# Sixteen groups of transposes read float32r copies made by DMAs, in a one-core decoder trunk

## The chip, the core and the metric

The kernel runs on one core of a Trainium2 chip. The metric is the device time of one execution in microseconds (us). The kernel before took 1412.33 us, the median of three runs (1411.7 to 1413.66). One core's engines work side by side, each through its own instructions in its own order: TensorE (PE, with its weight loads as PEld), VectorE (DVE), ScalarE (ACT), GpSimd (POOL) and SyncE (SP). In this kernel SP and POOL issue the DMAs. An instruction starts when the one before it on its engine has been issued and the data that it needs are there.

## What is computed

The reference is a trunk of two layers over 512 tokens of width 1024, all in float32. Each layer is a token mixer, a normalization, an MLP with a squared ReLU, a second normalization and a gate:

```python
for i in range(DEPTH):                       # DEPTH = 2
    mix = ssd_mixer(x, ...) if i % 2 == 0 else hgrn2_mixer(x, ...)
    h = layer_norm(DEEPNORM_ALPHA * x + mix, ln_g[i, 0], ln_b[i, 0])
    h = layer_norm(DEEPNORM_ALPHA * h + sq_relu_mlp(h, mlp_w1[i], mlp_w2[i]), ln_g[i, 1], ln_b[i, 1])
    x = h + jax.nn.sigmoid(h @ ple_w_gate[i]) * (p[i] @ ple_w_proj[i])
```

Both mixers begin with a projection of x and end with an output projection; the MLP is 1024 to 4096 to 1024.

## The kernel before

**Rows and columns.** The running state is the tile `acc`: for each of four chunks of 128 tokens, one row block of 128 partitions (tokens) by 1024 channels in float32. Norms and gates work on row blocks, since their sums go along the channels. The matrix products that follow need the channels on the partitions, so every normalized row block is transposed on TensorE: eight 128x128 squares for each chunk, four into one PSUM bank at a time. Such a group of four, with one identity matrix (`ident`, a slice of the constants `cst`), is what the profile shows as one row `pt<-cst,acc ... x4`. From the bank, ACT copies the group to the high part of a split operand and DVE takes the rest.

**Split products.** Every float32 product is made of three float32r ones (`mm3`, L120 to L122): both operands are split into a float32r high part (`hi`, by an ACT copy that rounds) and a float32r rest (`lo`, by a DVE subtraction). The profile writes `f32` for both types on TensorE; what is float32r there has `whi`, `wlo` or `b` (the tag `b8`) as its operands, what is float32 has `cst`, `acc`, `xw`, `qd` and the like.

**The norms in front of the MLPs.** `norm(0)` follows the first layer's output projection, `norm(2)` the second's. `out_project` goes chunk by chunk: two halves of the product (`out_part`, DVE adds each into `acc`, L260 or its like), then `after(c)`, which is `layer_norm`: statistics (L207, L208 in `norm(0)`), then two passes over the whole row block, `(x - mean) * g` (L223) and `* rs + b` (L224). Then `transpose_split` transposes the row block in two groups (L238), each followed by the ACT copy (L242) and the DVE subtraction (L243). The transposes of chunk c stand on TensorE in the middle of the products of the next chunk. `norm(1)` and `norm(3)` stand in front of the gates and go through the same `transpose_split`.

**The gate of the first layer** goes by halves h of the channels and chunks c. For each (h, c) there are 24 products into a bank, a sigmoid on ACT, a multiplication and the addition into `acc` on DVE (L666). The sum is the second layer's input, so it is transposed too: `turn(h, c)` (L625) is put off by one block through the list `late`, that is, it stands on TensorE behind the products of the next block. The last one, `turn(1, 3)`, is handed to the second layer's first products.

**What sets the order.** The program is written in a high-level order and a scheduler places each instruction on its engine's queue; `tc.high_priority(offset=...)` (the constants SOON = 40, LEAD = 100) moves pieces ahead. Tiles come from pools by tag; a tag has as many buffers as the phase's table says (`ssd`, `mlp0`, `hgrn`, `mlp1`), one where it says nothing. A new tile in a used buffer waits for the readers of the old one.

**POOL's queue.** POOL does almost nothing but issue DMAs: the loads of weight blocks `r` (`weight_sums`, L329), 512 KB each, in eights. The first eight of each MLP are the first blocks that DVE adds and subtracts (L336 and its neighbours) for the products of the first MLP group. SP's queue loads all other weights (`raw`).

Of the kernel before, what the change touches and what calls it, by code (L numbers as in the profile page):

```python
# [9 lines left out]
F32R = mybir.dt.float32r  # L10
# [5 lines left out]
P = 128  # L16
T = 512
# [27 lines left out]
def trunk(ctx: ExitStack, tc, a):  # L45
    nc = tc.nc
    pool = lambda name, bufs, **kw: ctx.enter_context(tc.tile_pool(name=name, bufs=bufs, **kw))
    cpool = pool("consts", 1)
# [15 lines left out]
    def nm(s):  # L64
        uid[0] += 1
        return f"{s}_{uid[0]}"

    def mk(p, shape, tag, dt=F32, **kw):
        return p.tile(list(shape), dt, tag=tag, name=nm(tag), **kw)

    def f32(t):
        return t.bitcast(F32)
# [16 lines left out]
    def tmp(tag, shape, dt=F32):  # L89
        return mk(phase[0], shape, tag, dt, bufs=phase[2].get(tag, 1))  # L90

    def bank(p, tag):
        return mk(p, [P, T], tag)
# [8 lines left out]
    def unit(src, lead=LEAD, after=None):  # L102
        n = src.shape[1]
        with tc.high_priority(offset=lead):
            raw = mk(raws, [P, 1024], "raw")
            nc.sync.dma_start(raw[:, :n], src)
        return split(raw[:, :n], lead, after)
# [39 lines left out]
    acc = mk(accp, [P, NCH, D], "acc")  # L147
# [32 lines left out]
    ident, triu, eps = cols["ident"], cols["triu"], cols["eps"]  # L180
    convw = cols["convw"].rearrange("p (i k) -> p i k", k=4)
    convb, dskip, snw, hlb, hnw = (cols[n] for n in ("convb", "dskip", "snw", "hlb", "hnw"))
    dtc = cols["dtc"]
    ones = tmp("cm", [P, P])
    nc.gpsimd.memset(ones, 1.0)
    one = mk(cpool, [P, 1], "one")
    nc.gpsimd.memset(one, 1.0)
    ones_s = mk(cpool, [P, 64], "ones_s")
    nc.gpsimd.memset(ones_s, 1.0 / 512)


    def ln_params(i):
        g = mk(w4, [P, D], "a")
        b = mk(w4, [P, D], "b")
        nc.sync.dma_start(g, a["ln"][2 * i : 2 * i + 1, :].to_broadcast([P, D]))
        nc.sync.dma_start(b, a["ln"][2 * i + 1 : 2 * i + 2, :].to_broadcast([P, D]))
        return g, b

    def layer_norm(i, c, gb, sums=None):

        src = acc[:, c, :]
        mv = mk(sm, [P, 2], "lnmv")
        sd = mk(sm, [P, 1], "lnsd")
        if sums is None:
            st = mk(sm, [P, 2, 6], "lnst")
            for h in range(2):
                nc.vector.bn_stats(st[:, h, :], src[:, h * 512 : (h + 1) * 512])  # L207
            nc.vector.bn_aggr(mv, st.rearrange("p a b -> p (a b)"))  # L208
            nc.scalar.activation(sd, mv[:, 1:2], AF.Sqrt, bias=eps)
        else:  # L210

            sq = mk(sm, [P, 2], "lnsq")
            nc.vector.tensor_scalar(mv[:, 0:1], sums[:, c, 0:1], sums[:, c, 1:2], -1.0 / D, ALU.add, ALU.mult)
            for h in range(2):
                nc.scalar.activation(
                    tmp("cbm" if i == 2 else "sg", [P, T]), src[:, h * 512 : (h + 1) * 512], AF.Square, bias=mv[:, 0:1], accum_out=sq[:, h : h + 1]
                )
            nc.vector.tensor_add(mv[:, 1:2], sq[:, 0:1], sq[:, 1:2])
            nc.scalar.activation(sd, mv[:, 1:2], AF.Sqrt, scale=1.0 / D, bias=eps)
        rs = mk(sm, [P, 1], "lnrs")  # L220
        nc.vector.reciprocal(rs, sd)
        shift = ALU.subtract if sums is None else ALU.add
        nc.vector.scalar_tensor_tensor(src, src, mv[:, 0:1], gb[0], shift, ALU.mult)  # L223
        nc.vector.scalar_tensor_tensor(src, src, rs, gb[1], ALU.mult, ALU.add)  # L224
# [3 lines left out]
    def behind(ins):  # L228
        return tc.issue_after(ins.ins) if ins is not None else nullcontext()

    def transpose_split(src, dst, c, apart, keep=None):

        sl = slice(c * P, (c + 1) * P)
        for q in range(2):
            pt = bank(psm, "pm") if (c == 3 if keep is not None else apart and q) else bank(pst, "pt")
            for j in range(4):
                k = 4 * q + j
                nc.tensor.transpose(pt[:, j * P : (j + 1) * P], src[:, k * P : (k + 1) * P], ident)  # L238
            v = pt.rearrange("p (j t) -> p j t", j=4)
            h = dst.hi[q][:, :, sl]  # L240
            with tc.high_priority(offset=LEAD if apart or keep is not None else SOON):
                nc.scalar.copy(h, v)  # L242
                turned_last[:] = [nc.vector.tensor_sub(dst.lo[q][:, :, sl], v, f32(h))]  # L243
                if keep is not None and q == 0:
                    nc.scalar.copy(keep[:, c // 2, :, c % 2 * P : (c % 2 + 1) * P], v)
            yield
# [38 lines left out]
    def norm(i, keep=None):  # L285

        gb = ln_params(i)
        h_s = Split(8)
        sums = mk(sm, [P, NCH, 2], "lnsum") if i else None

        def chunk(c):
            with tc.high_priority(offset=LEAD if c == 3 and i % 2 == 0 else 0 if c > 1 and i == 1 else SOON):
                layer_norm(i, c, gb, sums)

        return h_s, chunk, lambda c: transpose_split(acc[:, c, :], h_s, c, c == 3 and i % 2 == 0, keep), sums

# [259 lines left out]
    def mlp_and_gate(layer, h_s, last):  # L558
# [36 lines left out]
        for g, period in enumerate(PERIODS):  # L595
            if g < 4:
                tiles = hidden(g)
            if g > 0:
                if g == 4:
                    kept = tmp("blk", [P, 2, 4, 256]) if last else None  # L600
                    h_s, after, turned, sums = norm(2 * layer + 1, kept)
# [15 lines left out]
        rows = [tmp("blk", [P, 2, 4, 256]) for _ in range(2)]  # L617
        late = []

        def turn(h, c):  # L620

            sl = slice(c * P, (c + 1) * P)
            pt = bank(pst, "pt")
            for j in range(4):
                nc.tensor.transpose(pt[:, j * P : (j + 1) * P], acc[:, c, h * 512 + j * P : h * 512 + (j + 1) * P], ident)  # L625
            v = pt.rearrange("p (j t) -> p j t", j=4)
            hh = x_n.hi[h][:, :, sl]
            nc.scalar.copy(hh, v)
            nc.scalar.copy(rows[c // 2][:, h, :, c % 2 * P : (c % 2 + 1) * P], v)
            nc.vector.tensor_sub(x_n.lo[h][:, :, sl], v, f32(hh))  # L630
# [3 lines left out]
        def proj(c, pu):  # L634

            ps = pps[c] = bank(*((psj, "pj") if c > 1 and pps else (psy, "py%d" % (c % 2))))
            sl = slice(c * P, (c + 1) * P)
            for k in range(2):
                ks = slice(k * 512, (k + 1) * 512)
                mm3(ps, p_s[0][:, k, sl], p_s[1][:, k, sl], pu[0][:, ks], pu[1][:, ks], k == 0, k == 1)  # L640

        for h in range(2):
            pu = unit(a[f"wp_{layer}"][h])
            gu = [unit(a[f"wg_{layer}"][4 * h + j]) for j in range(4)]
            for c in range(NCH):
                sl = slice(c * P, (c + 1) * P)
                if h == c == 0:
                    turns = turned(1)
                    for i in range(NCH):
                        proj(i, pu)  # L650
                        if i in (1, 2):
                            next(turns)
                if h == 1:
                    proj(c, pu)
                turns = turned(c + 2) if h == 0 and c < 2 else None
                pg = bank(psj, "pj")
                sg = tmp("sg", [P, T])
                for k in range(8):
                    ks = slice((k % 2) * 512, (k % 2 + 1) * 512)
                    mm3(pg, h_s.h(k, sl), h_s.l(k, sl), gu[k // 2][0][:, ks], gu[k // 2][1][:, ks], k == 0, k == 7)  # L660
                    if turns and k in (2, 5):
                        next(turns)
                nc.scalar.activation(sg, pg, AF.Sigmoid)
                nc.vector.tensor_mul(sg, pps.pop(c), sg)
                d = acc[:, c, h * 512 : (h + 1) * 512]
                nc.vector.tensor_add(d, sg, d)  # L666
                while late:
                    late.pop(0)()
                late.append(lambda h=h, c=c: turn(h, c))
        return x_n, rows, late  # L670

    def values4(xs, rows, late):
# [297 lines left out]
    for j in range(17):  # L970
# [6 lines left out]
        if pend is not None:  # L977
            i = j - 1
# [27 lines left out]
    x_s, rows, late = mlp_and_gate(0, h_s, False)  # L1006
# [98 lines left out]
    def need(*key):  # L1105
        while key not in made:
            next(bg)
        return made[key]
# [218 lines left out]
    with tc.manual_schedule(engines={mybir.EngineType.PE}):  # L1327
        for h in range(0, 8, 2):
            if h % 4 == 0:
                halves.append(Split(4))  # L1330
            if h == 0:
                need("qf", 1)
                fill(AHEAD)
            scale = 1.0 if h < 6 else LAST
            for n in hcore(h, halves[-1], h % 4):
                fill(n * scale)
        for _ in bg:
            pass
    h_s, *after = norm(2)
    out_project(a["who"][4:8], halves[1], False, *after)  # L1340
    begin("mlp1")
    mlp_and_gate(1, h_s, True)
    phase[1].__exit__(None, None, None)

# [119 lines left out]
```

## Time and profile before

| | |
|---|---|
| device time, three runs | 1411.7, 1412.33, 1413.66 us |
| span of the profiled execution | 1409.6 us, 2.7 us under the median; the page has no other time of that execution |
| PE busy | 1404.3 us, 100%, 8001 instructions |
| DVE busy | 1069.1 us, 76% |
| ACT busy | 763.6 us, 54% |
| POOL busy | 45.8 us, 3%, 92 instructions |
| DMA | 181.69 MB, mean 129 GB/s |

How to read it: a row of a timeline gives an instruction's start and its duration in us, its engine and line, what it writes and reads, and the shapes. Matmuls are pipelined, so their durations overlap, and the distance between two starts is what one costs. The norms' transposes in question lie near 356 to 366 us and 1008 to 1018 us of the span, the gate's between 721 and 766 us.

### The profile page before, as it was taken

Reading aid. Unit: us, or ns where it says so; the run is one execution under the profiler, and the core shown is the slowest. Engines: PE = TensorE matmul, PEld = TensorE weight load, DVE = VectorE, ACT = ScalarE, POOL = GpSimd, SP = SyncE. Lnnn points to the kernel's source line nnn. Section 1 sums busy time; section 2 is a strip of 40 time slices with the busy share of each in tenths; the row PEclk is TensorE's granted clock in tenths of the full one; section 3 lists DMA queues with packets and bytes.
Section 4 is the critical chain, followed back from the end, with each engine's and each line's share of the span. In section 5 each row is a group of like instructions: output and inputs, shape, how many; then the busy total and the mean of one; then the engine's idle time right before and its main releaser. Section 6 shows DMA issues by size and latency. Waiting matters only on the chain.

```text
span 1409.6 us, 20400 instructions
## 1 busy us (share of the span) xinstructions
PE 1404.3 (100%) x8001; PEld 1168.1 (83%) x8001; DVE 1069.1 (76%) x1778; ACT 763.6 (54%) x1156; POOL 45.8 (3%) x92
## 2 busy tenths in 40 slices
PE   9999999999999999999999999999999999999998
PEld 7888888888988888888888888888898888888887
DVE  7989688698977668677986577678785867667795
ACT  7766465573354444545555547655555454544573
POOL 0000000001000000000000000000100000000100
PEclk9999999999999999999999999999999999999999
DMA  8433333234433444345621421222443444444731
GB/s 313 135 117 120 106 120 110 85 100 156 141 113 127 157 131 152 129 142 178 209 90 49 134 91 61 76 87 96 150 135 105 147 137 148 144 137 159 202 106 60
DMA packets 50399, 181.69 MB, mean 129 GB/s; under 512 B 5632, under 2 KB 6400, under 8 KB 50176
## 3 DMA queue, kind: packets, MB, share of 16 engines
q1 hardware_dynamic: 38784, 138.45, 29.6%
q0 software_dynamic: 11520, 41.95, 9.2%
q8 instruction: 63, 1.03, 0.3%
q14 instruction: 32, 0.26, 0.1%
HBM read 177.16 MB, written 2.16 MB: 127 GB/s over the span
## 4 chain that ended last, share of the span: by engine, by line
PE 99%; DMA 0%; DVE 0%; issue 0%; DVEq 0%
PE pj L120 25%; PE pj L121 25%; PE pj L122 25%; PE py L120 5%; PE py L122 5%; PE py L121 5%; PE py L906 1%; PE pt L238 1%; PE py L1175 1%; PE pm L923 1%; PE pm L871 1%; PE py L1301 1%; PE pt L859 0%; PE py L1303 0%; PE py L1240 0%; PE py L832 0%
## 5 line engine op out<-in xcount | busy, mean ns | idle before, releaser
L113 ACT CAST whi<-raw 128x1024 fp32r<-128x1024 f32 x218 | 228.8, 1050 | 333.2 <-PE pj L121 243.6
L120 PE MATMUL pj<-b,whi 128*128 128x512 f32 (+1 forms) x990 | 378.6, 383 | 0.0
L122 PE MATMUL pj<-b,wlo 128*128 128x512 f32 (+1 forms) x990 | 376.8, 381 | 0.0
L121 PE MATMUL pj<-b,whi 128*128 128x512 f32 (+1 forms) x990 | 376.6, 381 | 0.0
L116 DVE TENSOR_TENSOR wlo<-raw,whi 128x1024 fp32r<-128x1024 f32 x218 | 265.4, 1221 | 129.4 <-ACT whi L113 128.2
L121 PEld LDWEIGHTS pj<-b,whi 128*128 128x128 f32 x990 | 186.4, 188 | 34.6 <-issue 0.9
L122 PEld LDWEIGHTS pj<-b,wlo 128*128 128x128 f32 x990 | 186.3, 188 | 34.5
L120 PEld LDWEIGHTS pj<-b,whi 128*128 128x128 f32 x990 | 186.1, 188 | 34.0
L122 PE MATMUL pj<-whi,b 128*128 128x512 f32 x520 | 204.1, 392 | 0.0
L120 PE MATMUL pj<-whi,b 128*128 128x512 f32 x508 | 202.1, 398 | 0.0
L121 PE MATMUL pj<-wlo,b 128*128 128x512 f32 x508 | 199.2, 392 | 0.0
L113 ACT CAST whi<-r 128x1024 fp32r<-128x1024 f32 x76 | 80.0, 1053 | 68.5 <-PE pj L122 39.4
L122 PEld LDWEIGHTS pj<-whi,b 128*128 128x128 f32 x520 | 97.7, 188 | 20.1
L120 PEld LDWEIGHTS pj<-whi,b 128*128 128x128 f32 x508 | 95.5, 188 | 19.1 <-ACT b L1322 0.3
L121 PEld LDWEIGHTS pj<-wlo,b 128*128 128x128 f32 x508 | 95.5, 188 | 18.7 <-issue 0.2
L116 DVE TENSOR_TENSOR wlo<-r,whi 128x1024 fp32r<-128x1024 f32 x76 | 92.5, 1220 | 19.6 <-ACT whi L113 19.1
L122 PE MATMUL py<-whi,b 128*128 128x512 f32 x260 | 101.3, 390 | 0.0
L121 PE MATMUL py<-wlo,b 128*128 128x512 f32 x248 | 96.6, 389 | 0.0
L120 PE MATMUL py<-whi,b 128*128 128x512 f32 x248 | 96.4, 390 | 0.0
L329 POOL DMA_DIRECT2D r<-in_w x64 | 34.0, 532 | 1098.8 <-DVE wlo L116 544.3
L122 PEld LDWEIGHTS py<-whi,b 128*128 128x128 f32 x260 | 48.8, 188 | 10.2
L800 DVE SCALAR_TENSOR_TENSOR cv<-pj,cst,cv 128x509 f32<-128x509 f32 (+2 forms) x66 | 48.9, 746 | 10.6 <-ACT cv L797 9.8
(368 smaller groups left out, 1943.5 us busy)
## 6 DMA issues: line engine op xcount, KB each, us to landing
raw<-in_w SPq DMA_DIRECT2D x112, 512.0 KB, 3.3
r<-in_w POOLq DMA_DIRECT2D x64, 512.0 KB, 3.8
raw<-in_wssd SPq DMA_DIRECT2D x36, 512.0 KB, 3.9
a<-csd SPq DMA_DIRECT2D x16, 512.0 KB, 4.1
raw<-in_wso SPq DMA_DIRECT2D x16, 512.0 KB, 3.3
raw<-in_whq SPq DMA_DIRECT2D x16, 512.0 KB, 3.4
raw<-in_wg SPq DMA_DIRECT2D x15, 512.0 KB, 4.0
raw<-in_whvg SPq DMA_DIRECT2D x14, 512.0 KB, 3.4
```

The costliest lines, as they stand in the source:

```text
L113: nc.scalar.copy(hi[:, :n], f)
L116: nc.vector.tensor_sub(lo[:, :n], f, f32(hi[:, :n]))
L120: nc.tensor.matmul(out, sh, mh, start=start, stop=False, **kw)
L121: nc.tensor.matmul(out, sh, ml, start=False, stop=False, **kw)
L122: return nc.tensor.matmul(out, sl, mh, start=False, stop=stop, **kw)
L238: nc.tensor.transpose(pt[:, j * P : (j + 1) * P], src[:, k * P : (k + 1) * P], ident)
L329: queue.dma_start(t[i][u], src)
L800: nc.vector.scalar_tensor_tensor(cv[:, d:], ps[:, : T - d], convw[:, i, k : k + 1], cv[:, d:], ALU.mult, ALU.add)
L871: nc.tensor.matmul(pst_[:, c * P : (c + 1) * P], btok[:, c, :], xw[:, c].rearrange("p h q -> p (h q)"), start=True, stop=True)
L906: mm = nc.tensor.matmul(yds[0][64 * r : 64 * r + 64, sl], xdt[:, 2 * c + r, :], m[:, r, sl], start=True, stop=True)
L923: mm = nc.tensor.matmul(yo[:, c * P : (c + 1) * P], pv[:, c - 1].rearrange("p h q -> p (h q)"), cm[:, c * P : (c + 1) * P], start=True, st ...
L1175: nc.tensor.matmul(pcs[r][bs, at : at + n], kk[r][:, ts], qs, start=True, stop=True)
```

## The change

Sixteen of the groups of four transposes read another tile. They are the groups of chunks 0 and 1 behind `norm(0)` and `norm(2)` (two for each chunk, eight in all) and the eight groups of the first layer's gate. As soon as the float32 half row block (128x512, 256 KB) is final in `acc`, a DMA on POOL's queue copies it within SBUF into a tile of type float32r, with the bits unchanged (`same_bits`). The transposes read that tile, with an identity that POOL has cast to float32r (`rounded`), and write float32r into the PSUM bank; the ACT copy and the DVE subtraction behind them are as before. Chunks 2 and 3 of these norms and the norms in front of the gates are transposed from `acc` in float32, as before. The copies of the norms go to tag `xs` (four buffers in both phases), those of the gate to a new tag `xr`, which has one buffer.

```diff
+    def rounded(tag):
+        t = tmp(tag, [P, P], F32R)
+        nc.gpsimd.tensor_copy(t, ident)
+        return t
+
+    def same_bits(tag, src):
+        t = tmp(tag, [P, T], F32R)
+        nc.gpsimd.dma_start(f32(t), src)
+        return t
+
+    eye = [rounded("identr")]
...
-    ones_s = mk(cpool, [P, 64], "ones_s")
+    ones_s = tmp("ones_s", [P, 64])
...
-    def transpose_split(src, dst, c, apart, keep=None):
+    def transpose_split(src, dst, c, apart, keep=None, copies=None):
...
-                nc.tensor.transpose(pt[:, j * P : (j + 1) * P], src[:, k * P : (k + 1) * P], ident)
+                to = pt[:, j * P : (j + 1) * P]
+                if copies:
+                    nc.tensor.transpose(to.bitcast(F32R), copies[q][:, j * P : (j + 1) * P], eye[0])
+                else:
+                    nc.tensor.transpose(to, src[:, k * P : (k + 1) * P], ident)
...
                 layer_norm(i, c, gb, sums)
-
-        return h_s, chunk, lambda c: transpose_split(acc[:, c, :], h_s, c, c == 3 and i % 2 == 0, keep), sums
+                if i % 2 == 0 and c < 2:
+                    copies[c] = [same_bits("xs", acc[:, c, q * T : (q + 1) * T]) for q in range(2)]
+
+        return h_s, chunk, lambda c: transpose_split(acc[:, c, :], h_s, c, c == 3 and i % 2 == 0, keep, copies.get(c)), sums
...
+        eye[:] = [rounded("identr")]
+
-        def turn(h, c):
+        def turn(h, c, copy):
...
-                nc.tensor.transpose(pt[:, j * P : (j + 1) * P], acc[:, c, h * 512 + j * P : h * 512 + (j + 1) * P], ident)
+                nc.tensor.transpose(pt[:, j * P : (j + 1) * P].bitcast(F32R), copy[:, j * P : (j + 1) * P], eye[0])
...
-                late.append(lambda h=h, c=c: turn(h, c))
+                late.append(lambda h=h, c=c, copy=same_bits("xr", d): turn(h, c, copy))
...
+    eye[:] = [rounded("scb")]
     h_s, *after = norm(2)
```

The scheduler moves the transposes on TensorE. Here is the first group of chunk 0 behind `norm(0)`, in the stream of TensorE; `pj` is the bank of an output product, `b` its stationary operand, `whi` and `wlo` the split weights. Before:

```order
L120 MATMUL pj_3233<-whi_3162,b_446_2578 128x512
L121 MATMUL pj_3233<-wlo_3164,b_446_2578 128x512
L238 MATMUL pt_3205<-cst_165,acc_99 128x128 x4
L122 MATMUL pj_3233<-whi_3162,b_447_2579 128x512
L120 MATMUL pj_3272<-whi_3144,b_446_2578 128x512
```

and now, in the changed program, where the line of the transposes from a copy is L251:

```order
L120 MATMUL pj_3282<-whi_3152,b_447_2580 128x512
L121 MATMUL pj_3282<-wlo_3154,b_447_2580 128x512
L251 MATMUL pt_3211<-identr_167,xs_3207 128x128 x4
L122 MATMUL pj_3282<-whi_3152,b_448_2581 128x512
L120 MATMUL pj_3296<-whi_3158,b_447_2580 128x512
```

The group now stands twelve product matmuls further back in the stream (behind 1696 of them from the program's start, 1684 before): in the next half product, `pj_3282`, which is the one called `pj_3272` above. Counted in the same way, the other groups of the norms stand 12, 9 and 9 further back in `norm(0)` and 12, 12, 10 and 15 in `norm(2)`; the gate's eight groups keep their places among the products.

On DVE, around the second pass over chunk 1 of `norm(0)` (L224 before, L235 now; L243 and L258 are the subtractions behind the transposes). Before:

```order
L223 SCALAR_TENSOR_TENSOR acc_99<-acc_99,lnmv_3247,a_3122 128x1024
L243 TENSOR_TENSOR b_553_3129<-pt_3212,b_551_3127 128x4x128
L221 RECIPROCAL lnrs_3254<-lnsd_3248 128x1
L260 SCALAR_TENSOR_TENSOR acc_99<-pj_3272,ri_3139,acc_99 128x512
L224 SCALAR_TENSOR_TENSOR acc_99<-acc_99,lnrs_3254,b_3123 128x1024
L207 BN_STATS lnst_3302<-acc_99 128x6
```

and now:

```order
L234 SCALAR_TENSOR_TENSOR acc_99<-acc_99,lnmv_3253,a_3124 128x1024
L232 RECIPROCAL lnrs_3260<-lnsd_3254 128x1
L275 SCALAR_TENSOR_TENSOR acc_99<-pj_3282,ri_3141,acc_99 128x512
L258 TENSOR_TENSOR b_553_3130<-pt_3211,b_551_3128 128x4x128
L235 SCALAR_TENSOR_TENSOR acc_99<-acc_99,lnrs_3260,b_3125 128x1024
L218 BN_STATS lnst_3312<-acc_99 128x6
L258 TENSOR_TENSOR b_554_3131<-pt_3218,b_552_3129 128x4x128
```

Both subtractions of chunk 0 stood ahead of the second pass over chunk 1; now the first stands just in front of it and the second behind it.

On POOL, the start of its queue in the first layer. Before:

```order
L189 MEMSET ones_s_171 128x64
L329 DMA r_3840<-in_w_0 128x1024
L329 DMA r_3834<-in_w_0 128x1024
L329 DMA r_3836<-in_w_0 128x1024
L329 DMA r_3841<-in_w_0 128x1024
```

and now:

```order
L200 MEMSET ones_s_173 128x64
L186 CAST identr_167<-cst_165 128x128
L191 DMA xs_3207<-acc_99 128x512
L191 DMA xs_3209<-acc_99 128x512
L191 DMA xs_3264<-acc_99 128x512
L191 DMA xs_3266<-acc_99 128x512
L348 DMA r_3850<-in_w_0 128x1024
L348 DMA r_3844<-in_w_0 128x1024
```

The four copies stand in front of the first eight loads of the MLP's weight blocks. The second layer has the same on POOL (four copies in front of eight loads), and the gate has eight copies there one by one. SP's queue keeps its order.

More of the change, by code (lines that the diff above doesn't have):

```diff
@@ L289, in norm @@
         sums = mk(sm, [P, NCH, 2], "lnsum") if i else None
+        copies = {}
         def chunk(c):
```

## The prediction

> **What bounds the kernel.** I began with the page of the kernel before, its engines and the chain of work that ended last:
>
> ```profile
> span 1409.6 us, 20400 instructions
> PE 1404.3 (100%) x8001; PEld 1168.1 (83%) x8001; DVE 1069.1 (76%) x1778; ACT 763.6 (54%) x1156; POOL 45.8 (3%) x92
> PE 99%; DMA 0%; DVE 0%; issue 0%; DVEq 0%
> ```
>
> TensorE makes up 99% of the chain, and in the whole span it is without work for 1409.6 - 1404.3 = 5.3 us. So a microsecond of TensorE's own work taken away shortens the kernel by one, a new wait of TensorE lengthens it by its length, and work elsewhere counts only where TensorE comes to wait for it. Next I read TensorE's timeline (start, duration, engine, line, shapes) around a group of transposes:
>
> ```profile
> 362.52 0.39 PE L122 MATMUL pj<-whi,b 128*128 128x512 f32 x1
> 362.97 0.39 PE L121 MATMUL pj<-wlo,b 128*128 128x512 f32 x1
> 363.20 0.60 PE L238 MATMUL pt<-cst,acc 128*128 128x128 f32 x4
> 363.56 0.48 PE L122 MATMUL pj<-whi,b 128*128 128x512 f32 x1
> 363.88 0.40 PE L120 MATMUL pj<-whi,b 128*128 128x512 f32 x1
> ...
> 369.13 0.28 PE L120 MATMUL pj<-b,whi 128*128 128x256 f32 x1
> 369.37 0.28 PE L122 MATMUL pj<-b,wlo 128*128 128x256 f32 x1
> ```
>
> Two products of 512 columns start 0.45 us apart at the top (one lies between), so a step is 0.227 us. From 362.97 to 363.88 are 0.91 us with two products in them; the rest, 0.45 us, is what a group of four float32 transposes costs, 0.11 us each. Products of 256 columns step by 0.12 us.
>
> **What a float32r transpose costs.** No row of before has one. Groups by shape (busy us, mean ns of one, idle before) give durations with the columns that stream:
>
> ```profile
> L122 PE MATMUL pj<-whi,b 128*128 128x512 f32 x520 | 204.1, 392 | 0.0
> L121 PE MATMUL pj<-b,whi 128*128 128x256 f32 x96 | 27.2, 285 | 0.0
> L871 PE MATMUL pm<-xw,btok 128*128 128x128 f32 x96 | 13.4, 275 | 0.0
> L1175 PE MATMUL py<-qd,cv 128*32 128x88 f32 x256 | 5.7, 241 | 0.0
> ```
>
> float32r: (392 - 285) / 256 = 0.42 ns a column. float32: (275 - 241) / 40 = 0.85, twice that; 128 columns of it are 0.11 us, just the measured step. So the float32 transposes are set by the 128 columns of the identity that stream, and float32r would halve that if the law holds at 128 columns. Extending the two float32r steps, 0.227 at 512 and 0.12 at 256, gives 0.067 at 128; by the column alone it is 0.054. A group falls from 0.45 to 0.27 us (0.22 by columns): 0.18 us, times 16 groups = **-2.9 us** (at most -3.7). I take the steps, since they hold the overhead too. The other end is no gain, since each matmul also loads its stationary operand, here the copy:
>
> ```profile
> L906 PEld LDWEIGHTS py<-b,xdt 128*64 128x64 f32 x256 | 14.0, 137 | 1.7 <-issue 0.4 <-DVE pv L881 0.4
> L238 PEld LDWEIGHTS pt<-cst,acc 128*128 128x128 f32 x112 | 12.9, 140 | 4.1 <-issue 0.9 <-DVE b L243 0.6 <-ACT blk L245 0.4
> L871 PEld LDWEIGHTS pm<-xw,btok 128*128 128x128 f32 x96 | 12.2, 190 | 2.4 <-DVE xw L866 1.9 <-issue 0.2
> ```
>
> From 64 to 128 columns a load of a product grows by 53 ns, 0.83 ns a column, or 106 ns for 128. At that pace four transposes would still cost 0.43 us. But a transpose's load of 128 columns takes 140 ns, as long as a product's of 64, so I take its pace as 53 ns and the load as no bound. [...]
>
> **When the copies land.** The transposes used to need `acc` alone; now each group waits for a DMA of 256 KB that starts when DVE has written the half. No DMA of this kind is in before. The nearest (KB each, us from issue to landing) are, on the whole program's list:
>
> ```profile
> r<-in_w POOLq DMA_DIRECT2D x64, 512.0 KB, 3.8
> raw<-in_w SPq DMA_DIRECT2D x112, 512.0 KB, 3.3
> out<-acc SPq DMA_DIRECT2D x7, 256.0 KB, 2.0
> r<-r POOLq DMA_DIRECT2D x2, 512.0 KB, 5.6
> ```
>
> The ends are 2.0 us (the right size, on SP's queue) and 5.6 us (the right queue, SBUF to SBUF, double the size, in traffic). On SP half the bytes take 1.3 us less; from POOL's 3.8 that leaves 2.5, and with a semaphore's wake on either side, DVE to POOL and DMA to TensorE, I take **2.8 us** from DVE's end to TensorE's start. [...]
>
> **Norms.** DVE's second pass, and the first group of the row block behind it, for chunks 0 and 1 of `norm(0)`, then of `norm(2)`:
>
> ```profile
> 354.73 1.28 DVE L224 SCALAR_TENSOR_TENSOR acc<-acc,lnrs,b 128x1024 f32<-128x1024 f32 x1
> 361.75 1.28 DVE L224 SCALAR_TENSOR_TENSOR acc<-acc,lnrs,b 128x1024 f32<-128x1024 f32 x1
> 1006.96 1.28 DVE L224 SCALAR_TENSOR_TENSOR acc<-acc,lnrs,b 128x1024 f32<-128x1024 f32 x1
> 1013.63 1.28 DVE L224 SCALAR_TENSOR_TENSOR acc<-acc,lnrs,b 128x1024 f32<-128x1024 f32 x1
> ```
>
> ```profile
> 356.10 0.63 PE L238 MATMUL pt<-cst,acc 128*128 128x128 f32 x4
> 1008.39 0.63 PE L238 MATMUL pt<-cst,acc 128*128 128x128 f32 x4
> 1015.06 0.63 PE L238 MATMUL pt<-cst,acc 128*128 128x128 f32 x4
> ```
>
> Before, the group started 0.1 to 0.2 us behind the pass, which held TensorE up by 0.15 us in all at the two chunks 0; that goes. Now the groups stand 12, 9, 12 and 10 steps of 0.227 us later in the stream: 2.7, 2.0, 2.7 and 2.3 us. Copy ready against arrival: chunk 0 of `norm(0)` 356.01 + 2.8 = 358.8 against 358.8, no wait; chunk 1 363.03 + 2.8 = 365.8 against 363.20 + 2.04 = 365.2, 0.6, less the 0.3 by which cheaper transposes let the pass itself start earlier: 0.3. `norm(2)`: chunk 0 1011.04 against 1011.1, 0.05 with its spread; chunk 1 1017.7 against 1017.3, 0.3 by the same reckoning. Together **+0.65 us**. Behind a waiting group stand the out-projection's products; ACT and DVE then get the block later, while the MLP's first products need it only after chunk 2.
>
> **Gate.** The additions that end the second, the third and the last of the eight blocks, and the turns of the first, the second, the third and the last:
>
> ```profile
> 720.87 0.69 DVE L666 TENSOR_TENSOR acc<-sg,acc 128x512 f32<-128x512 f32 x1
> 726.22 0.69 DVE L666 TENSOR_TENSOR acc<-sg,acc 128x512 f32<-128x512 f32 x1
> 763.42 0.69 DVE L666 TENSOR_TENSOR acc<-sg,acc 128x512 f32<-128x512 f32 x1
> ```
>
> ```profile
> 721.47 0.60 PE L625 MATMUL pt<-cst,acc 128*128 128x128 f32 x4
> 724.67 0.60 PE L625 MATMUL pt<-cst,acc 128*128 128x128 f32 x4
> 730.59 0.60 PE L625 MATMUL pt<-cst,acc 128*128 128x128 f32 x4
> 765.83 0.60 PE L625 MATMUL pt<-cst,acc 128*128 128x128 f32 x4
> 764.00:768.00 4.00, 4.00 (x21) 3.31 (x20) 1.93 (x4) 3.02 (x5) 0.00 (x0) 1.00 0.37 129
> ```
>
> A turn comes one block behind its addition. The third block's copy has from 726.91 to 730.59, 3.7 us, and that is the least among six of the eight. Two are short. The second block is final at 721.56, but tag `xr` has one buffer: its copy can start only when the first turn, at 721.47, has read it, about 721.9, and lands at 724.7 against an arrival of 724.5: 0.2. The last block is final at 764.11; 2.8 later is 766.9 against 765.65: 1.3, and the window's row (second number from the end: the DMA engines 37% busy with weights) lets me add 0.2. **+1.7 us.**
>
> **At nothing.** POOL's casts of the identity precede everything. The four copies stand ahead of the eight loads of `r`, which now start with chunk 1's copy, at 363.0, instead of at 345.67 or before (an x7 row holds seven loads):
>
> ```profile
> 345.67 3.65 POOL L329 DMA_DIRECT2D r<-in_w  x7 [7.54 <-PE pt L953]
> 382.70 1.22 DVE L336 TENSOR_TENSOR r<-r,r 128x1024 f32<-128x1024 f32 x1
> 1033.94 1.22 DVE L336 TENSOR_TENSOR r<-r,r 128x1024 f32<-128x1024 f32 x1
> ```
>
> Eight times 512 KB from 363 at the 316 GB/s that such a burst moved below are some 14 us, done by 378, before DVE's first use at 382.70. The cover is 5 us; without it the wait falls on DVE, then on the MLP's products. In `norm(2)` chunk 1's copies go at 1014.9, 14 us more make 1029, and the first use is at 1033.94: 5 us too.
>
> ```profile
> 345.00:360.00 15.00, 15.00 (x80) 12.27 (x77) 12.40 (x19) 2.62 (x6) 3.65 (x7) 1.00 0.79 316
> ```
>
> **Sum:** -2.9 (rate) + 0.65 (norms) + 1.7 (gate) - 0.15 (old waits) = -0.7 us. From the span 1409.6 to 1408.9; as the median of the runs lies 2.7 above the span, 1412.3 - 0.7 = **1411.6 us**.
>
> **Rivals.** (1) *The copies come late* (slower): each microsecond of latency above 2.8 is paid at six places, since each group of a chunk waits for nearly the same landing: two chunks in each of two norms and two turns, 6 us per us. At 2.9 us the sum is zero, from 3.3 us on it passes +0.2%, at 3.6 us it is -0.7 + 4.8 = +4.1: 1416.4. [...] Against it: SP's 2.0.
>
> (2) *The rate does not change*, since the load binds at 106 ns: -0.3 + 2.35 - 0.15 = +1.9, 1414.2. [...] Against it stands the 140 ns row.
>
> (3) *All hidden*: 2.3 us of latency and the gain by columns. The norms' waits go, the gate keeps 0.7: -3.7 + 0.7 - 0.15 = -3.1, 1409.2. For it: the 2.0 us row.
>
> **Chances.** Forecast 0.50, late copies 0.20, rate unchanged 0.17, all hidden 0.13. The forecast's own range is 1410.1 to 1413.0 (0.25 us of latency either way at six places); with the others' sides 1409.2 to 1416.4. A change of 0.2%, 2.8 us, is about what a measurement of this kernel can tell from none. Faster by that: rival 3 and a little of the forecast, 0.18; slower: most of rival 1 and some of rival 2, 0.20; the same 0.62.
>
> **What would show it.** On TensorE, groups of L251 and L646 costing 0.27 us: right; 0.43: rival 2. Waits of TensorE on a POOL DMA in front of those lines: some 0.3 us at the chunks 1 and 1.5 us at the last turn. From issue to landing of `xs` and `xr`: 2.5 us; 3.3 is rival 1. DVE waiting for `r` at its first additions of weight blocks, or the MLP's first groups waiting for `b8`, would make the whole wrong.

## The result, and the profile after

The changed kernel takes 1429.47 us (median of four runs, 1426.25 to 1433.04) against 1412.62 before: a ratio of 1.0122, 95% interval 1.011 to 1.0134, 17 us slower. The prediction, 1411.6 us in a range from 1409.2 to 1416.4, was wrong. The page of the changed kernel:

```profile
span 1427.4 us, 20459 instructions
PE 1410.7 (99%) x8001; PEld 1172.7 (82%) x8001; DVE 1069.9 (75%) x1778; ACT 764.6 (54%) x1156; POOL 55.9 (4%) x111
PE 72%; issue 24%; DMA 2%; DVE 1%; ACT 0%; POOLq 0%; DVEq 0%; ACTq 0%
```

TensorE now has 16.7 us without work, 5.3 before, and its busy time has grown by 6.4 us although it executes the same number of instructions. Its waits (line, releaser; us in total, times, longest):

```profile
PE pt L253 <- DVE b L258: 7.3, 2, 4.5
PE pt L646 <- DMA xr<-acc: 3.1, 2, 1.7
PE pt L251 <- DMA xs<-acc: 1.3, 2, 0.9
```

The two largest are not waits on copies. L253 is the float32 transpose from `acc`, of chunk 2, which waits for DVE to empty the bank `pt`. Where the time went is best seen by matching the product matmuls (L120 to L122) of both timelines by their number and taking the difference of their starts, here in us, after minus before (worked out from the two traces):

```
stretch                                     lag at its start   at its end   lost
start of the program                              0.0             0.8        0.8
up to the transposes of norm(0)                   0.8             0.8        0.0
norm(0), chunks 0 and 1                           0.8             1.2        0.4
entry of the first MLP (370 to 389 of before)     1.2             6.9        5.7
first MLP                                         6.9             6.9        0.0
first gate                                        6.9             9.8        2.9
second layer's mixer                              9.8             9.8        0.0
norm(2), chunks 0 and 1                           9.8            10.7        0.9
entry of the second MLP (1022 to 1033)           10.7            17.7        7.0
the rest                                         17.7            17.8        0.1
```

The 0.8 us at the start are there in e2 below too and not in e1, which has the same start, so they are no part of the change. Some 13 of the 17 us are lost at the two entries of the MLPs, behind the norms, and three in the gate.

**The entry of the first MLP.** ACT's timeline in this stretch, of before:

```profile
370.48 1.05 ACT L113 CAST whi<-raw 128x1024 fp32r<-128x1024 f32 x1 [1.45 <-DMA raw<-in_w]
371.62 0.59 ACT L242 CAST b<-pt 128x512 fp32r<-128x512 f32 x1
```

and of the changed kernel, with DVE's and TensorE's rows that follow from it:

```profile
376.86 1.04 ACT L113 CAST whi<-raw 128x1024 fp32r<-128x1024 f32 x1 [6.53 <-DMA raw<-in_w]
377.81 0.58 ACT L257 CAST b<-pt 128x512 fp32r<-128x512 f32 x1
...
378.42 0.69 DVE L258 TENSOR_TENSOR b<-pt,b 128x512 fp32r<-128x512 f32 x1 [3.15 <-ACT b L257]
...
373.10 0.60 PE L253 MATMUL pt<-cst,acc 128*128 128x128 f32 x4
379.17 1.12 PE L253 MATMUL pt<-cst,acc 128*128 128x128 f32 x4 [2.83 <-DVE b L258]
380.73 0.41 PE L120 MATMUL pj<-b,whi 128*128 128x256 f32 x1
```

The cast of a raw weight block waits 6.53 us for its load. The copy of chunk 2's first group (L257), whose transposes were done by 373.7, stands behind it in ACT's queue and starts at 377.81; DVE follows at 378.42; only then is the one bank `pt` free for the second group, and TensorE has idled for 2.83 us. The DMA issues between 355 and 385 us say why the load is late (KB each, median us from issue to landing). Of before, and then of the changed kernel:

```profile
raw<-in_w SPq DMA_DIRECT2D x4, 512.0 KB, 3.4
```

```profile
r<-in_w POOLq DMA_DIRECT2D x8, 512.0 KB, 10.1
xs<-acc POOLq DMA_DIRECT2D x4, 256.0 KB, 2.5
raw<-in_w SPq DMA_DIRECT2D x2, 512.0 KB, 8.1
```

The eight `r` loads, pushed behind the copies, are now in this stretch, and the two raw loads take 8.1 us beside them (median); the one that the cast waits for leaves at 367.82 and lands at 376.78, 9.0 us later. The other half of the loss is in the last PE row: a product of 256 columns lasts 0.41 us, 0.28 before. Windows of the changed kernel (busy us and count of PE, PEld, DVE, ACT, POOL; granted clock of TensorE; DMA share; GB/s):

```profile
372.00:379.00 7.00, 4.34 (x37) 4.13 (x35) 3.85 (x5) 1.53 (x2) 0.00 (x0) 0.95 1.03 416
379.00:386.00 7.00, 6.83 (x36) 6.83 (x37) 3.47 (x6) 1.17 (x3) 0.00 (x0) 0.56 0.38 149
```

Behind the idle stretch TensorE runs at a granted clock of about half until 385. So the wait costs 2.83 us and the slow stretch about as much again: 5.7.

**The entry of the second MLP** has the same wait, but there was a second cause. In the kernel before, ACT cast this raw block behind chunk 2's second group:

```profile
1025.71 0.59 ACT L242 CAST b<-pt 128x512 fp32r<-128x512 f32 x1
...
1026.39 1.04 ACT L113 CAST whi<-raw 128x1024 fp32r<-128x1024 f32 x1
```

In the changed kernel the scheduler has put the cast ahead of chunk 3's statistics (L226) and of the copies of both groups of chunk 2 (L257). The statistics and the first group's copy wait for the late load, and TensorE's second group waits until that copy and DVE's subtraction have emptied the bank:

```profile
1036.95 1.04 ACT L113 CAST whi<-raw 128x1024 fp32r<-128x1024 f32 x1 [4.79 <-DMA raw<-in_w]
1037.90 0.72 ACT L226 ACTIVATE cbm<-acc,lnmv 128x512 f32<-128x512 f32 x1
...
1039.32 0.56 ACT L257 CAST b<-pt 128x512 fp32r<-128x512 f32 x1
...
1041.51 1.11 PE L253 MATMUL pt<-cst,acc 128*128 128x128 f32 x4 [4.46 <-DVE b L258]
```

**The gate.** TensorE waits for two copies, those of chunk 3 in either half (POOL's issue, then TensorE's group):

```profile
741.08 0.54 POOL L191 DMA_DIRECT2D xr<-acc  x1 [6.13 <-DMA raw<-in_whvg]
746.36 0.51 PE L646 MATMUL pt<-identr,xr 128*128 128x128 f32 x4 [1.65 <-DMA xr<-acc]
...
773.03 0.54 POOL L191 DMA_DIRECT2D xr<-acc  x1 [8.80 <-PE py L122]
775.72 0.51 PE L646 MATMUL pt<-identr,xr 128*128 128x128 f32 x4 [1.43 <-DMA xr<-acc]
```

**What a float32r group costs** shows in TensorE's rows around one of them:

```profile
362.37 0.39 PE L121 MATMUL pj<-wlo,b 128*128 128x512 f32 x1
362.60 0.46 PE L251 MATMUL pt<-identr,xs 128*128 128x128 f32 x4
362.90 0.47 PE L122 MATMUL pj<-whi,b 128*128 128x512 f32 x1
363.20 0.40 PE L120 MATMUL pj<-whi,b 128*128 128x512 f32 x1
```

From 362.37 to 363.20 are 0.83 us, less two steps of 0.227: 0.38 us, where a float32 group takes 0.45. The gain is 0.07 us a group, about 1.1 us in all.

### The profile page after: what moved, and what is told of

It reads as the page before. It is cut to its first block, busy times and chain, and to the rows that moved or that the text cites. A ratio compares the mean times of both kernels' runs of the same rounds, so it can differ in the third digit from the quotient of the medians.

```text
span 1427.4 us, 20459 instructions
## 1 busy us (share of the span) xinstructions
PE 1410.7 (99%) x8001; PEld 1172.7 (82%) x8001; DVE 1069.9 (75%) x1778; ACT 764.6 (54%) x1156; POOL 55.9 (4%) x111
## 3 DMA queue, kind: packets, MB, share of 16 engines
q8 instruction: 63, 1.03, 0.3%
## 4 chain that ended last, share of the span: by engine, by line
PE 72%; issue 24%; DMA 2%; DVE 1%; ACT 0%; POOLq 0%; DVEq 0%; ACTq 0%
PE pj L120 17%; PE pj L122 17%; PE pj L121 17%; PE py L120 5%; PE py L121 5%; PE py L122 5%; DMA raw<-in_w 1%; PE py L1196 1%; PE pt L253 1%; DMA xr<-acc 1%; PE py L1322 0%; DMA xs<-acc 0%; PE py L1324 0%; PE py L1261 0%; DMA acc<-in_xw 0%
## 5 line engine op out<-in xcount | busy, mean ns | idle before, releaser
L120 PE MATMUL pj<-b,whi 128*128 128x512 f32 (+1 forms) x990 | 379.8, 385 | 0.0
L122 PE MATMUL pj<-b,wlo 128*128 128x512 f32 (+1 forms) x990 | 378.4, 382 | 0.0
L121 PE MATMUL pj<-b,whi 128*128 128x512 f32 (+1 forms) x990 | 378.3, 382 | 0.0
L122 PEld LDWEIGHTS pj<-b,wlo 128*128 128x128 f32 x990 | 188.1, 190 | 34.4
L120 PEld LDWEIGHTS pj<-b,whi 128*128 128x128 f32 x990 | 187.7, 190 | 34.2
L122 PE MATMUL pj<-whi,b 128*128 128x512 f32 x520 | 203.9, 392 | 0.0
L120 PE MATMUL pj<-whi,b 128*128 128x512 f32 x508 | 201.9, 397 | 0.0
L122 PEld LDWEIGHTS pj<-whi,b 128*128 128x128 f32 x520 | 97.6, 188 | 20.1
L120 PEld LDWEIGHTS pj<-whi,b 128*128 128x128 f32 x508 | 95.5, 188 | 19.2 <-ACT b L1343 0.3
L122 PE MATMUL py<-whi,b 128*128 128x512 f32 x260 | 101.2, 389 | 0.0
L120 PE MATMUL py<-whi,b 128*128 128x512 f32 x248 | 96.4, 390 | 0.0
L122 PEld LDWEIGHTS py<-whi,b 128*128 128x128 f32 x260 | 48.8, 188 | 10.2
L120 PEld LDWEIGHTS py<-whi,b 128*128 128x128 f32 x248 | 46.5, 188 | 10.2 <-DVE sg L685 0.3
```

The lines of the kernel that those rows point to most:

```text
L120: nc.tensor.matmul(out, sh, mh, start=start, stop=False, **kw)
L121: nc.tensor.matmul(out, sh, ml, start=False, stop=False, **kw)
L122: return nc.tensor.matmul(out, sl, mh, start=False, stop=stop, **kw)
```

## The experiments

Theory A, formed on these rows: the displaced `r` loads collide with a raw load whose cast blocks ACT. Theory B, the rival of the prediction that had the right sign: the copies themselves come late. The first four runs go with the kernel before at 1412.19 us (15 runs on the same chip), e5 to e7 with 1412.15 (27 runs).

**e1, the norms alone.**

```diff
-                late.append(lambda h=h, c=c, copy=same_bits("xr", d): turn(h, c, copy))
+                late.append(lambda h=h, c=c: turn(h, c, None))
...
-                nc.tensor.transpose(pt[:, j * P : (j + 1) * P].bitcast(F32R), copy[:, j * P : (j + 1) * P], eye[0])
+                nc.tensor.transpose(pt[:, j * P : (j + 1) * P], acc[:, c, h * 512 + j * P : h * 512 + (j + 1) * P], ident)
```

> The change at the norms alone; the gate is transposed from acc in float32 as before. Theory A (displaced loads): the eight weight loads r that now stand behind the copies on POOL's queue start with chunk 1's copy instead of 16 us earlier, share the DMA engines with the one raw load that ACT casts next, that cast blocks ACT's queue, and TensorE runs dry at the entry of each MLP. In the changed kernel this cost about 6 us in the first layer and 8 in the second, so this run should keep some 13 to 15 of the 17 us: 1425 to 1428, with TensorE waits of 2 us and more in front of the transposes of chunk 2. Theory B (the rival of the prediction: late copies, paid at the groups that wait for them): the waits on the copies at the norms were 0.4 and 0.9 us in the changed kernel, so this run should be within 1.5 us of before: 1412 to 1414.

Measured: 1422.52 us, ratio 1.0076 (1.0059 to 1.0093), +10.3 us. Its waits are as theory A has them, its size is not:

```profile
PE pt L253 <- DVE b L258: 6.9, 2, 4.2
```

At the first MLP it loses 3.1 us where the changed kernel loses 5.7. The wait is nearly the same, but the clock stays up, as TensorE's timeline and then a window behind the wait show:

```profile
378.31 0.66 PE L253 MATMUL pt<-cst,acc 128*128 128x128 f32 x4 [2.78 <-DVE b L258]
```

```profile
379.00:382.00 3.00, 3.00 (x26) 2.86 (x26) 2.55 (x4) 0.59 (x1) 0.00 (x0) 1.00 0.61 240
```

**e2, the gate alone.**

```diff
-                if i % 2 == 0 and c < 2:
+                if False:
```

> The change at the gate alone; the norms are transposed from acc in float32 as before, and no copy stands in front of the r loads. Theory A: no loss at the entries of the MLPs; the gate's own two waits on its copies (1.65 and 1.5 us in the changed kernel), less eight cheaper groups of some 0.08 us, cost 2 to 3 us: 1414.5 to 1415.5. Theory B: the gate holds most of the late copies, so most of the 17 us should stay: above 1420.

Measured: 1418.41 us, ratio 1.0044 (1.0029 to 1.0059), +6.2 us: neither theory's number. No loss at the MLPs' entries, as A says, but the last copy came later than in the changed kernel, and behind TensorE's wait of 3.53 us the granted clock fell, to 0.64 in the mean of 772 to 776 us (timeline of POOL and TensorE, then a window):

```profile
766.63 0.54 POOL L191 DMA_DIRECT2D xr<-acc  x1 [8.79 <-DVE lmask L1037]
771.37 0.67 PE L646 MATMUL pt<-identr,xr 128*128 128x128 f32 x4 [3.53 <-DMA xr<-acc]
```

```profile
772.00:776.00 4.00, 4.00 (x13) 3.16 (x13) 1.82 (x2) 1.07 (x2) 0.00 (x0) 0.64 0.00 0
```

SP issues a raw load of 512 KB at 766.66, 0.03 us behind the copy of 256 KB, and the copy reaches TensorE 4.7 us after its issue instead of 2.7. The last turn costs 5.2 us here, the block of chunk 3 in the first half 1.4. That the load is what delays the copy is read from this trace; no run takes the load away. e1 and e2 add up to 16.5 of the 17 us, but by luck: the first MLP loses 3.1 us in e1 and 5.7 in the changed kernel, the gate 6.2 in e2 and 2.9 there.

**e3, late loads without any copy.** The kernel before, with

```diff
                 layer_norm(i, c, gb, sums)
+                if i % 2 == 0 and c in (1,):
+                    for _ in range(4):
+                        nc.gpsimd.tensor_copy(tmp("xs", [P, T])[:, 0:1], acc[:, c, 0:1])
```

> The kernel before, with four POOL copies of one column (128x1) that wait for the second norm pass of chunk 1 and stand in front of the eight r loads, behind norm(0) and norm(2). No DMA copies, every transpose in float32 from acc; the instructions of TensorE, DVE, ACT and SP stand in the order of before. Theory A: the r loads are as late as in the changed kernel, so the loss at the MLPs' entries comes without any copy: +10 to +15 us, 1422 to 1428, with the ACT cast of a raw block waiting 4 us or more for its DMA and TensorE waiting 2 us or more behind it. Theory B: no copies to wait for, so no loss: 1411.5 to 1413.5.

Measured: 1416.45 us, ratio 1.003 (1.0018 to 1.0041), +4.3 us. Against B, the loss at the first MLP comes without a copy, 3.0 us, by the same chain. First ACT and TensorE there, then ACT at the second MLP:

```profile
375.22 1.04 ACT L113 CAST whi<-raw 128x1024 fp32r<-128x1024 f32 x1 [6.22 <-DMA raw<-in_w]
376.17 0.58 ACT L242 CAST b<-pt 128x512 fp32r<-128x512 f32 x1
...
377.53 0.66 PE L238 MATMUL pt<-cst,acc 128*128 128x128 f32 x4 [2.73 <-DVE b L243]
...
1029.13 0.59 ACT L242 CAST b<-pt 128x512 fp32r<-128x512 f32 x1
...
1031.89 1.05 ACT L113 CAST whi<-raw 128x1024 fp32r<-128x1024 f32 x1 [1.98 <-DMA raw<-in_w]
```

At the second MLP the load is late too, but in this kernel ACT has the old order: the cast stands behind chunk 2's second group, delays nobody, and nothing is lost. So A in its first form, late loads alone, was too simple. In the second layer it takes the late load and the cast's new place. (The traced execution loses another 1.1 us elsewhere, 0.4 in front of the gate and 0.7 at the program's end, which this chain does not explain.)

**e4, the loads seven us earlier.** As e3, with `c in (0,)`.

> As the run before, but the four one-column POOL copies wait for chunk 0's second norm pass, so the r loads start near 356 us of the span instead of 363. The eight loads took some 11 us in the changed kernel, so they end near 367, when the raw load that was late there is issued. Theory A in the form that the collision with this one raw load is what counts: little or no loss, 1412 to 1414.5. Theory A in the form that the loads are late for their own first use (DVE at 383 us): none either here, so a loss of 3 us or more would speak against both and for something that the POOL instructions do by themselves. Theory B: no loss.

Measured: 1412.41 us, ratio 1.0003 (0.9994 to 1.0013): no loss. The loads leave some 12 us later than before (357.3 instead of 345.7). They were not through near 367, as expected, but at 371.3: the last four landed between 367.4 and 371.3, and the raw load had left at 367.36. It took 5.2 us, not 9.0, and TensorE did not come to wait. So it is enough that most of the burst is over by then; how much must be, these runs do not show.

**e5, e1 with the copies on SP's queue.** Against e1:

```diff
-                    copies[c] = [same_bits("xs", acc[:, c, q * T : (q + 1) * T]) for q in range(2)]
+                    t = mk(w4, [P, D], "ab"[c], F32R)
+                    copies[c] = [t[:, q * T : (q + 1) * T] for q in range(2)]
+                    for q in range(2):
+                        nc.sync.dma_start(f32(copies[c][q]), acc[:, c, q * T : (q + 1) * T])
```

> As e1 (the change at the norms alone), but the eight copies go by SP's queue into buffers of the pool w4, so that nothing stands in front of the r loads on POOL. The order of TensorE, DVE and ACT is that of e1, its ACT order included, in which behind norm(2) the cast of a raw block stands ahead of chunk 3's statistics and of the second copy of chunk 2. Theory A (late r loads collide with a raw load whose ACT cast blocks what is behind it): the r loads are in time again, so both losses of e1 (3 us at the first MLP, 8 us at the second) go: 1411.5 to 1413.5. Rival C (the new order on ACT alone costs the 8 us of the second layer, whatever the r loads do): 1418 to 1421. Theory B (the copies' own latency): the waits on copies stay near 0.8 us in all and with them 1412 to 1414, which does not tell it from A; the TensorE waits in front of chunk 2 do.

Measured: 1411.47 us, ratio 0.9998 (0.9989 to 1.0007): all 10.3 us of e1 are gone, with ACT's order as in e1, so rival C falls. The cast that waited 6.5 us waits 0.93, and TensorE has no wait on a copy or in front of chunk 2. ACT's row, and then the issues of 355 to 385 us:

```profile
370.08 1.05 ACT L113 CAST whi<-raw 128x1024 fp32r<-128x1024 f32 x1 [0.93 <-DMA raw<-in_w]
```

```profile
raw<-in_w SPq DMA_DIRECT2D x4, 512.0 KB, 3.2
a<-acc SPq DMA_DIRECT2D x2, 256.0 KB, 2.4
```

With before, e3 and e1 this makes a square for the second MLP: loads in time and old order 0, loads late and old order 0 (e3), loads in time and new order 0 (e5), loads late and new order 6.3 us (e1).

**e6, the gate without the copies of chunk 3.** Against e2:

```diff
-                late.append(lambda h=h, c=c, copy=same_bits("xr", d): turn(h, c, copy))
+                late.append(lambda h=h, c=c, copy=same_bits("xr", d) if c < 3 else None: turn(h, c, copy))
...
+                if copy is None:
+                    nc.tensor.transpose(pt[:, j * P : (j + 1) * P], acc[:, c, h * 512 + j * P : h * 512 + (j + 1) * P], ident)
```

> As e2 (the change at the gate alone), but the blocks of chunk 3 in both halves are transposed from acc in float32 as before; six of eight blocks keep the copy. In e2 TensorE waited for the copies of just these two blocks, 1.2 and 3.5 us, and ran at a granted clock of 0.64 behind the longer wait. Theory A (two copies that share the DMA engines with a weight load are late, the other six are hidden): the loss of e2 goes: 1411.3 to 1413. Theory B (every copy of the gate costs something): two of eight go, so some 4.5 of the 6.2 us stay: 1416 to 1417.

Measured: 1412.43 us, ratio 1.0002 (0.9993 to 1.0011). The loss is gone with two of the eight copies; the six others cost nothing.

**e7, e5 and e6 together.**

> e5 and e6 together: 14 of the 16 groups read float32r copies, the norms' copies on SP's queue, the gate's on POOL's, chunk 3 of the gate in float32. If the losses of the changed kernel are the two collisions that e5 and e6 take away, what is left is the gain on TensorE, 0.08 us a group (0.37 against 0.45 us) or 1.1 us, less about 0.8 us of waits on the norms' copies: 1411.5 to 1412.5, not to be told from before. The prediction's term of 0.18 us a group would make it 2.5 - 0.8 = 1.7 us: 1410.5.

Measured: 1411.92 us, ratio 0.9998 (0.9989 to 1.0007): not to be told from before, and neither is the difference between the two sizes of the group's gain. In the matched timelines its last products lie 0.6 us ahead of before; fourteen groups by 0.07 us would be 1.0. No version beat the kernel before by more than a measurement can tell.

**e8, groups of twelve.** Against e6:

```diff
-            for j in range(4):
+            for j in list(range(4)) * 3:
```

> As e6, but every transpose of the gate's groups is issued three times over into the same place of the bank: twelve in a group instead of four, in six blocks float32r from the copies and in the two of chunk 3 float32 from acc. (The work is repeated; the result is the same.) It is read from TensorE's timeline, not from the time. A group of four cost 0.45 us in float32 and 0.38 in float32r, not the predicted 0.27. Theory D (the pace is halved nearly as predicted, and a fixed tail of some 0.09 us behind a float32r group, until the next product starts, eats the rest): eight more cost 8 x 0.11 = 0.87 us in float32 and 8 x 0.072 = 0.58 us in float32r, groups of 1.32 and 0.96 us. Theory E (the load of the stationary operand sets a pace near 0.09 to 0.1 us, so that the gain is small for every transpose): the float32r group comes to 1.1 us or more.

TensorE's rows, one float32r and one float32 group, each with the product ahead and the two behind:

```profile
721.62 0.40 PE L122 MATMUL pj<-whi,b 128*128 128x512 f32 x1
721.86 1.14 PE L649 MATMUL pt<-identr,xr 128*128 128x128 f32 x12
722.83 0.47 PE L120 MATMUL pj<-whi,b 128*128 128x512 f32 x1
723.14 0.40 PE L121 MATMUL pj<-wlo,b 128*128 128x512 f32 x1
...
739.87 0.39 PE L122 MATMUL pj<-whi,b 128*128 128x512 f32 x1
740.10 1.47 PE L647 MATMUL pt<-cst,acc 128*128 128x128 f32 x12
741.33 0.48 PE L120 MATMUL py<-whi,a 128*128 128x512 f32 x1
741.64 0.39 PE L121 MATMUL py<-wlo,a 128*128 128x512 f32 x1
```

Less two steps, twelve float32 transposes cost 1.77 - 0.45 = 1.32 us, as both theories say. Twelve in float32r cost 1.52 - 0.45 = 1.07 us: eight more than in a group of four cost 0.69, so 0.086 us each. That lies between D (0.96 us a group) and E (1.1 and more), nearer to E: a float32r transpose is a fifth cheaper than a float32 one, not a half. e8's one execution took 1417.47 us with the repeated work and is not compared. What sets 0.086 us was not found; the load takes 141 ns as in float32.

## Why the prediction was wrong, step by step

- **"At nothing": the `r` loads.** This is the step that failed. It checked the displaced loads against their own first use, and there it held: the last one landed at 383.0 instead of by 378, DVE first used one at 389.8, and DVE never became the bound. The sign named for this case, DVE waiting for `r`, therefore did not show. It did not ask what else needs the DMA engines in the stretch into which they move. Some 4 MB then shared them (DMA share 1.03 from 372 to 379 us) with one raw load, which took 9.0 us instead of 3.3 and whose cast stands in ACT's queue ahead of chunk 2's copies. Before had already shown that cast waiting 1.45 us for its DMA, the thinnest cover in the place. The two entries cost 5.7 and 7.0 us; e3 and e5 show the chain from both sides.
- **The change's effect on ACT's order was not counted.** The part on the norms followed TensorE, DVE and POOL. That the cast had moved ahead of chunk 2's copies and chunk 3's statistics in the second layer was to be read in the program's order beforehand; the square of e1, e3 and e5 shows that it decides there.
- **A wait was priced at its length.** Behind both waits at the MLPs' entries TensorE's clock fell: 2.83 us became 5.7 and 4.46 us 7.0. At the first entry that was bad luck: in e1 and e3 nearly the same wait left the clock up (last section).
- **The rate**, -2.9 us, was the right sign and mis-sized: 0.07 us a group instead of 0.18, -1.1 us. The law of 0.42 ns a column from 512 and 256 columns does not hold at 128 (e8: 0.086 us instead of 0.067). The rival "rate unchanged" was nearer: its 106 ns a load, drawn from the products' loads, is contradicted by the 86 ns of e8, as the 140 ns row had suggested, but it came closer to the sum than the row's extrapolation.
- **The norms' waits on copies** (+0.65) were 0.4 and 0.9 us, 1.3 in all, at chunk 0 of each norm instead of chunk 1. From issue to landing the copies of `norm(0)` took 2.5 us and those of `norm(2)` 3.0, but from the end of DVE's pass over chunk 0 to TensorE's start were 3.3 us there and 3.8 in `norm(2)`, where 2.8 had been taken. Of that 2.8, 0.3 us for the two ends was the author's estimate; POOL's issue alone came 0.7 us behind DVE's end (357.55 behind 356.82, 1018.75 behind 1018.08). A slip in this sum made no difference: for chunk 1 of `norm(2)` the reckoning used for chunk 1 of `norm(0)` gives 0.1 us (1017.7 - 1017.3, less 0.3), not 0.3.
- **The gate** (+1.7) came to 2.9 us in the changed kernel and 6.2 in e2. The last turn waited as forecast (1.43 against 1.5 us). The wait at the second block, for the one buffer of `xr`, did not come, and the fourth block, which was thought to have plenty of time, waited 1.65 us, with the loads of the next stage in flight beside its copy (the DMA engines were 68% busy from 734 to 745 us).
- **Late copies**, the rival on the slower side, had the right sign for another reason. Its price of 6 us for each us of latency was not what acted: e5 and e6 together keep 14 of the 16 groups and lose nothing. (By its own price its sum reaches +0.2% at 3.4 us of latency, not at 3.3.)

## What to carry to other kernels

When an edit puts waiting DMAs in front of others in one queue, follow the displaced transfers to where they land in time and list what shares the DMA engines with them there, not only who uses them first. Then look at what stands behind each consumer of those transfers in its engine's queue: here, at the second MLP, a late load cost nothing where its cast stood behind the work (e3) and 7.0 us where it stood in front of it (changed kernel). And compare the order of every engine, also of those that the edit does not touch.

## What the runs showed of the hardware

**A TensorE wait of 2.83 us cost 5.7 us in the changed kernel, one of 2.78 us cost 3.1 in e1.** The longest waits in these runs, with what the clock did (windows by half a microsecond, in e3 by three): 4.46 (changed kernel, second MLP), 4.15 (e1), 3.53 (e2) and 2.83 us (changed kernel, first MLP) were followed by a granted clock of 0.50; 2.78 (e1) and 2.73 us (e3) by 1.00. In the first MLP of the changed kernel the clock fell within the idle stretch, near 378.3 us, and came back near 385.1:

```profile
377.00:378.00 1.00, 0.00 (x0) 0.00 (x0) 0.00 (x0) 1.00 (x2) 0.00 (x0) 1.00 1.03 410
378.50:379.00 0.50, 0.00 (x0) 0.00 (x0) 0.50 (x1) 0.00 (x0) 0.00 (x0) 0.50 1.11 442
...
384.00:385.00 1.00, 1.00 (x7) 1.00 (x7) 0.00 (x0) 0.00 (x0) 0.00 (x0) 0.50 0.00 0
385.50:386.00 0.50, 0.50 (x7) 0.50 (x6) 0.00 (x0) 0.29 (x1) 0.00 (x0) 1.00 0.00 0
```

It stayed down for 6.8 us here and in the second MLP (e1 too), and for 3.4 in e2. The trace of the changed kernel records the granted clock with its times. Its changes there lie 372.05, 6.83, 655.36, 6.83 and 378.88 us apart, all whole multiples of 3.413 us (109, 2, 192, 2 and 111); the stays of e1 and e2 are two and one of it. With this step the three traces can be divided into pieces, each from a change of its own. The programs' ends left out, the pieces at whose ends the clock fell held 1.99 us without TensorE work (changed kernel, first MLP), 2.29 (e1), 3.30 (e2) and 3.41 (changed kernel, second MLP). The fullest pieces that were found without a fall held 1.65 us in the changed kernel's gate and 1.66 in e1, whose wait of 2.78 us fell into two pieces as 1.66 and 1.12. The pieces' edges lie differently in each execution: the first one behind the start of the span at 2.9 us in the changed kernel, 1.7 in e1 and 0.1 in e2. That it is the idle time within one piece, and not the length of the wait, that decides is the author's reading of these four falls; no run was made to show it. The stays of 6.8 us had 0.8 to 1.9 us of idle time in the piece behind the fall too, the one of 3.4 us had none. This may be why the four executions of the changed kernel lie 6.8 us apart and those of before 2.0; only one of the four is traced.

**A copy within SBUF by DMA** of 256 KB took 2.2 us from issue to landing in the gate of e6, 2.4 on SP's queue in e5, and on POOL's in the changed kernel 2.5 in `norm(0)` and 3.0 in `norm(2)` (medians); beside a load of 512 KB issued 0.03 us later it took 4.7 us until TensorE started (e2). A load of 512 KB on SP's queue took 9.0 us beside eight such loads on POOL's (changed kernel), and 3.3 before.
